# Two-layer hybrid encoder: the order of TensorE's matmuls through projections and branches

## The chip, the cores and the metric

The kernel runs on one core of a Trainium2 chip. The metric is device time in microseconds (us) of one execution. Each time is the median of several runs; a profile is one execution of the same program with the hardware profiler on.

## The reference

Two layers of a bidirectional encoder act on 272 tokens (16 meta tokens and 256 sequence tokens) of width 1024. Each layer projects the normalised tokens to four parallel mixers of width 256 and to a gate per mixer, adds the gated results, and goes through a feed-forward part of width 2816:

```python
for l in range(DEPTH):
    u = rms_norm(h, ln_mix[l])
    (aq, ak, av, bq, bk, bv, cq, ck, cv, dq, dzf, dzb, di, dg, gz) = split_in(u @ w_in[l])
    y_a = windowed_sink_attention(aq, ak, av, attn_sink[l], bias_a)
    y_b = axial_rope_attention(rms_norm(bq, qk_norm_q[l]), rms_norm(bk, qk_norm_k[l]), bv, row, col, key_ok)
    y_c = differential_attention(cq, ck, cv, lam, bias_c, key_ok, diff_subnorm[l], lam_init)
    y_d = hgrn2_bidirectional(dq, dzf, dzb, di, dg, lb_all[0, l], lb_all[1, l], valid, hgrn_out_norm[l])
    gate = sigmoid(gz).reshape(Bn, L, N_BRANCH, D_MODEL)
    merged = gate[:, :, 0] * (y_a @ w_branch[l, 0])
    for n, y in enumerate((y_b, y_c, y_d), start=1):
        merged = merged + gate[:, :, n] * (y @ w_branch[l, n])
    h = h + merged @ w_out[l]
    u = rms_norm(h, ln_ffn[l])
    h = h + (silu(u @ w_ffn_gate[l]) * (u @ w_ffn_up[l])) @ w_ffn_down[l]
return rms_norm(h, ln_final)[:, META_END:]
```

(Reshapes are left out.) Mixers a, b and c are softmax attentions with two key heads for four query heads; d is a gated linear recurrence that runs forwards and backwards. All values are float32.

## The kernel before, in words

**Tiles.** Activations are held transposed: 128 features on the partitions, 272 tokens along the row; a `slot` is 128 x 2 x 272. Weights come in blocks of 512 KB, 128 x 1024, in the order of the list `plan`. `split_next` (L258 to L279) issues the load of a block into `raw` on SP, ScalarE casts it to `whi` (L275), and VectorE writes the rest, raw minus `whi`, to `wlo` (L276). Activations are split into two parts in the same way. A product is then three matmuls, hi·a0, hi·a1 and lo·a0: `prod` (L290 to L292), or `prod_t` (L307 to L309) with the roles turned round, 512 columns at a time, in layer 1's gates and branch products. A column block, `block` (L294), is 8 such products or 24 matmuls into one PSUM tile of the pool `psm` (tiles `pmm`, four buffers). These are called the big matmuls here.

**Projections and branches.** A layer runs through 22 projections (`ORDER`, loop at L908), and then through gates and branch products (`MIXING` in layer 0, loop at L965; `mixing_t`, L830, in layer 1). Between these blocks stands the mixers' own work, written as two Python generators that `advance` (L900) takes one step further after each block:

- `branch_d` (L675) is the linear branch d. Its `close` (L690, matmuls L700 and L712) and `apart` (L718, L728) are many matmuls of 32 or 64 rows; then come L780 and L781, L794, L803, and at the end `mix` and `head_rstd`.
- `softmax_stream` (L623) does the branches c, b and a, for each query tile `scores` (L484, matmul L492), a softmax on VectorE and ScalarE, `turn` (L426, transposes L432 and L438), and per branch a `mix` (L410, matmuls L415 and L421). It lets `WAIT_C[l]` steps pass before it begins, and then waits for the branch's `ready`.

`values` (L388) transposes a projection of values (L395, and L404 for the meta tokens) and copies it to `vn` and `vm` (L396, L405); `prep_b` (L523) computes the norms of branch b's heads (`head_cols` L380, L541, `head_rstd` L371) and its rotation (L553); `mixing_t` ends each half with transposes of the sum `acc` (L868). All these use PSUM tiles of the pool `psa` (`pat`, four buffers).

**Order.** The program names its instructions in this order, with `values` and `prep_b` called right behind the projection that feeds them. A scheduler then orders each engine's instructions, by their place in the program and by when it expects their operands to be ready; the engines run that order as it stands, with waits on one another.

Of the kernel before, what the change touches and what calls it, by code (L numbers as in the profile page):

```python
# [15 lines left out]
P = 128  # L16
# [5 lines left out]
DEPTH = 2  # L22
# [20 lines left out]
BRANCHES = (3, 2, 1, 0)  # L43
AHEAD = 1
RATE_D, RATE_S = 1.0, 1.0
WAIT_C = (8, 8)


def mixing_order():
# [20 lines left out]
def first_token(l, name):  # L70

    return META if l == DEPTH - 1 and (name[1] in "qg" or name[:3] == "dzb") else 0
# [9 lines left out]
def trunk(ctx, tc, xT, w_in, w_branch, w_out, w_gate, w_up, w_down, rel_bias, params, consts, masks, onehot, ln_out, out):  # L82
    nc = tc.nc
    V, S, G, PE = nc.vector, nc.scalar, nc.gpsimd, nc.tensor

    one = ctx.enter_context(tc.tile_pool(name="one", bufs=1))
    wraw = ctx.enter_context(tc.tile_pool(name="wraw", bufs=5))
# [43 lines left out]
    def midt():  # L131
        return mid.tile([P, T], F32, tag="mid", name=nm("mid"))
# [694 lines left out]

    gl = ctx.enter_context(tc.tile_pool(name="gl", bufs=1))

    def mixing_t(acts, rcol, done, advance):  # L830

        gates, merged = {}, []
        acc = None
        for kind, b, half in MIXING_T:
            n = BRANCHES[b]
            if kind == "g":
                pss = [pmm(), pmm()]
                for x in range(4):
                    w = weights()
                    for k in range(2):  # L840
                        for i in range(2):
                            prod_t(pss[i], w, k * HALF, acts[2 * x + k], i, x + k == 0, x + k == 4)
                    advance(RATE_D, RATE_S)
                for i in range(2):
                    g = gates[n, half, i] = slot().rearrange("p a b -> p (a b)")[:, :HALF]
                    S.activation(out=g, in_=pss[i][:, :HALF], func=AF.Tanh, scale=rcol[:, i:i + 1])
                continue
            while n not in done:
                advance(1.0, 1.0)
            if acc is None:  # L850
                acc = accp.tile([P, KT, T], F32, tag="at", name=nm("acc")).rearrange("p a b -> p (a b)")[:, :2 * DM]
            w = weights()
            advance(RATE_D, RATE_S)
            for i in range(2):
                ps = pmm()
                for j in range(2):
                    prod_t(ps, w, j * HALF, done[n][j], i, j == 0, j == 1)
                g, a = gates[n, half, i], acc[:, DM * i + HALF * half:DM * i + HALF * (half + 1)]
                if b == 0:
                    V.scalar_tensor_tensor(out=a, in0=g, scalar=1.0, in1=ps[:, :HALF], op0=ALU.add, op1=ALU.mult)  # L860
                else:
                    V.scalar_tensor_tensor(out=g, in0=g, scalar=1.0, in1=ps[:, :HALF], op0=ALU.add, op1=ALU.mult)
                    V.tensor_tensor(out=a, in0=a, in1=g, op=ALU.add)
            if b == 3:
                for m in range(4 * half, 4 * half + 4):
                    ps = pat()
                    for i in range(2):
                        PE.transpose(ps[:, P * i:P * (i + 1)], acc[:, DM * i + P * m:DM * i + P * (m + 1)], ident)  # L868
                    t = slot(F32R)
                    S.copy(t[:, 0, META:], ps[:, :SEQ])  # L870
                    V.tensor_tensor(out=t[:, 1, META:], in0=ps[:, :SEQ], in1=t[:, 0, META:], op=ALU.subtract)
                    merged.append(t)
        return merged

    for l in range(DEPTH):
# [29 lines left out]
                    credit[x] -= 1.0  # L905
                    next(gen, None)

        for idx, name in enumerate(ORDER):  # L908
            t0 = first_token(l, name)
            ps = lead[idx] if idx < 3 else block(acts, t0)  # L910
            if l == 0 and idx == 3:
                prep_small()
            if name[:2] == "dz":
                d, j = name[2], int(name[3])
                z = midt()
                V.tensor_tensor(out=z[:, t0:], in0=ps[:, t0:T], in1=rstd[:, t0:], op=ALU.mult)
                dd = 0 if d == "f" else 1
                kdst, fdst = dt["KK"][:, 2 * dd + j, :], dt["T1"][:, 2 * (1 - dd) + j, :]
                if t0:
                    G.memset(kdst[:, :t0], 0.0)  # L920
                    G.memset(fdst[:, :t0], 1.0)
                fdst, kdst = fdst[:, t0:], kdst[:, t0:]
                S.activation(out=fdst, in_=z[:, t0:], func=AF.Sigmoid)
                S.activation(out=kdst, in_=z[:, t0:], func=AF.Sigmoid, scale=-1.0)
                if l > 0:
                    c = 2 * dd + j
                    V.tensor_scalar(out=fdst, in0=fdst, scalar1=lbc[:, c:c + 1], scalar2=lb[:, c:c + 1], op0=ALU.mult, op1=ALU.add)
                    V.tensor_scalar(out=kdst, in0=kdst, scalar1=lbc[:, c:c + 1], scalar2=None, op0=ALU.mult)
                V.tensor_scalar(out=fdst, in0=fdst, scalar1=1e-30, scalar2=None, op0=ALU.max)
                continue  # L930
            if name[0] == "d":
                dst = dt[name[1]][:, int(name[2]), :]
            else:
                half = 1 if name[1] == "v" or name[-1] == "1" else 0
                if half == 0:
                    cur = pj[name[:2]] = slot()
                dst = pj[name] = cur[:, half, :]
            scale = {"aq": 0.125, "cq": 32 ** -0.5, "dq": 0.125}.get(name[:2])
            if t0:
                G.memset(dst[:, :t0], 0.0)  # L940
            if scale is None:
                V.tensor_tensor(out=dst[:, t0:], in0=ps[:, t0:T], in1=rstd[:, t0:], op=ALU.mult)
            else:
                V.scalar_tensor_tensor(out=dst[:, t0:], in0=ps[:, t0:T], scalar=scale, in1=rstd[:, t0:], op0=ALU.mult, op1=ALU.mult)
            if name == "dg1":
                sg = gslot()
                S.activation(out=sg, in_=dt["g"], func=AF.Sigmoid)
                V.tensor_tensor(out=dt["g"], in0=dt["g"], in1=sg, op=ALU.mult)
            if name == "di1":
                dt["val", 3] = values([dt["i"][:, 0, :], dt["i"][:, 1, :]])  # L950
            if name[1] == "v":
                n = "abc".index(name[0])
                if n == 1:
                    prep_b(l, pj)
                    pj["b"] = parts_of(pj["bq"], pj["bk"])
                elif n == 2:
                    pj["c"] = parts_of(pj["cq"], pj["ck"], True)
                    if l == 0:
                        load_bias("a")
                pj["val", n] = values([pj[name]])  # L960
                pj["ready", n] = True
            advance(RATE_D if idx >= 8 else 0.0, RATE_S if idx >= 10 else 0.0)
        gates, merged = {}, []
        acc = w = None
        for kind, i, m in MIXING if l < DEPTH - 1 else ():  # L965
            n = BRANCHES[i]
            if kind == "g":

                if m % 2 == 0:
                    gates[n, m // 2] = slot()  # L970
                g = gates[n, m // 2][:, m % 2, c0:]
                ps = block(acts, c0)
                V.tensor_tensor(out=g, in0=ps[:, c0:T], in1=rstd[:, c0:], op=ALU.mult)  # L973
                S.activation(out=g, in_=g, func=AF.Tanh, scale=0.5)
                advance(RATE_D, RATE_S)
                continue
            while n not in done:
                advance(1.0, 1.0)
            if acc is None:
                acc = accp.tile([P, KT, T], F32, tag="at", name=nm("acc"))  # L980
            if m % 4 == 0:
                w = weights()
                advance(RATE_D, RATE_S)
            ps = pmm()
            for j in range(2):
                prod(ps, w, 2 * (m % 4) + j, done[n][j], c0, j == 0, j == 1)
            g = gates[n, m // 2][:, m % 2, c0:]
            if i == 0:
                V.scalar_tensor_tensor(out=acc[:, m, c0:], in0=g, scalar=1.0, in1=ps[:, c0:T], op0=ALU.add, op1=ALU.mult)
            else:  # L990
                t = midt()
                V.scalar_tensor_tensor(out=t[:, c0:], in0=g, scalar=1.0, in1=ps[:, c0:T], op0=ALU.add, op1=ALU.mult)
                V.tensor_tensor(out=acc[:, m, c0:], in0=acc[:, m, c0:], in1=t[:, c0:], op=ALU.add)
            if i == 3:
                merged.append(split_from(acc[:, m, :], c0, slot))
        if l == DEPTH - 1:
            merged = mixing_t(acts, rcol, done, advance)

            ws, pss = [weights(), weights()], [pmm(), pmm()]
            for k0 in (0, 4):  # L1000
# [195 lines left out]
```

## Time and profile before

| | |
|---|---|
| median of 3 runs | 924.46 us (923.78 to 926.39) |
| the profiled execution's own time | 924.85 us |
| its span in the profile | 923.1 us |
| its mean granted clock of TensorE | .995 |
| TensorE busy | 906.5 us (98%) |
| VectorE busy | 664.9 us (72%) |
| ScalarE busy | 505.1 us (55%) |

The span is what lies between the first and the last instruction of the profile. TensorE's rows are PE, its weight loads PEld, VectorE is DVE, ScalarE ACT, GpSimd POOL. `L395` is line 395 of the kernel; a row `pat L492 x6` is six matmuls of line 492 into tiles of the name `pat`. A number in brackets behind a row is idle time before it, with the instruction that ended it. The granted clock is a share of full speed.

### The profile page before, as it was taken

The numbers are of one execution on the slowest core, as the hardware profiler recorded it, in microseconds if no ns is written. First come the engines' busy times: TensorE is split into PE (matmuls) and PEld (weight loads), VectorE is DVE, ScalarE is ACT, GpSimd is POOL, SyncE is SP. The second block draws the span as 40 slices with busy tenths as digits, with TensorE's granted clock in tenths as the row PEclk, the third lists the DMA queues.
The fourth block names the chain that finished last, engine by engine and source line by source line (L and its number), as shares of the span: only waits on it lengthen the run. The fifth ranks groups of instructions, "written<-read, shape, count | busy, mean of one in ns | idle before, by whom it ended". The sixth has DMA issues, their size and how long they took to land.

```text
span 923.1 us, 18697 instructions
## 1 busy us (share of the span) xinstructions
PE 906.5 (98%) x7566; PEld 836.8 (91%) x7566; DVE 664.9 (72%) x1279; ACT 505.1 (55%) x852; POOL 23.5 (3%) x53
## 2 busy tenths in 40 slices
PE   7999999999999999999999999999999999999996
PEld 6988898999999999999999997787788999999885
DVE  7888886858987666665558888766577866777444
ACT  7645766555466444454446568675445655445432
POOL 1520000000000000000000000000000000000000
PEclk9999999999999999999999999999999999999998
DMA  8942344445454555555555423545465655555551
GB/s 314 247 145 77 108 138 138 137 138 158 140 183 161 182 174 171 181 171 174 182 176 168 150 82 115 166 132 162 157 195 152 201 182 173 189 186 184 186 179 45
DMA packets 42614, 150.04 MB, mean 163 GB/s; under 512 B 5024, under 2 KB 5696, under 8 KB 42528
## 3 DMA queue, kind: packets, MB, share of 16 engines
q1 hardware_dynamic: 40896, 144.84, 48.2%
q0 software_dynamic: 1344, 3.48, 1.5%
q8 instruction: 59, 0.97, 0.4%
q10 hardware_dynamic: 288, 0.52, 0.2%
q14 instruction: 27, 0.22, 0.1%
HBM read 147.22 MB, written 1.61 MB: 161 GB/s over the span
## 4 chain that ended last, share of the span: by engine, by line
PE 94%; DVE 3%; ACT 1%; issue 1%; DMA 1%; SPq 0%; DVEq 0%; ACTq 0%
PE pmm L290 22%; PE pmm L292 22%; PE pmm L291 22%; PE pmm L307 6%; PE pmm L309 6%; PE pmm L308 6%; PE pat L492 2%; PE pat L421 2%; PE pat L432 1%; DVE wlo L276 1%; ACT whi L275 1%; PE pat L700 1%; PE pat L371 1%; PE pat L415 1%; DMA h<-in_xT_dram 1%
## 5 line engine op out<-in xcount | busy, mean ns | idle before, releaser
L275 ACT CAST whi<-raw 128x1024 fp32r<-128x1024 f32 (+1 forms) x275 | 285.1, 1040 | 329.6 <-PE pmm L291 157.4
L290 PE MATMUL pmm<-slot,whi 128*128 128x272 f32 (+1 forms) x1552 | 449.8, 290 | 5.8 <-ACT slot L324 5.2
L291 PE MATMUL pmm<-slot,whi 128*128 128x272 f32 (+1 forms) x1552 | 446.2, 288 | 0.1
L292 PE MATMUL pmm<-slot,wlo 128*128 128x272 f32 (+1 forms) x1552 | 446.0, 288 | 0.1
L276 DVE TENSOR_TENSOR wlo<-raw,whi 128x1024 fp32r<-128x1024 f32 (+1 forms) x275 | 332.5, 1211 | 116.7 <-ACT whi L275 113.3
L290 PEld LDWEIGHTS pmm<-slot,whi 128*128 128x128 f32 x1552 | 293.5, 189 | 12.4 <-ACT slot L324 5.5
L291 PEld LDWEIGHTS pmm<-slot,whi 128*128 128x128 f32 x1552 | 294.2, 190 | 2.1 <-DVE slot L325 1.1
L292 PEld LDWEIGHTS pmm<-slot,wlo 128*128 128x128 f32 x1552 | 293.6, 189 | 1.9 <-issue 0.5
L307 PE MATMUL pmm<-whi,slot 128*128 128x512 f32 x184 | 73.2, 398 | 0.0
L309 PE MATMUL pmm<-wlo,slot 128*128 128x512 f32 x184 | 73.0, 397 | 0.0
L308 PE MATMUL pmm<-whi,slot 128*128 128x512 f32 x184 | 72.2, 392 | 0.0
L307 PEld LDWEIGHTS pmm<-whi,slot 128*128 128x128 f32 x184 | 34.6, 188 | 8.9 <-issue 1.2
L308 PEld LDWEIGHTS pmm<-whi,slot 128*128 128x128 f32 x184 | 34.6, 188 | 7.7
L309 PEld LDWEIGHTS pmm<-wlo,slot 128*128 128x128 f32 x184 | 34.6, 188 | 7.7 <-issue 0.3
L1030 DVE TENSOR_TENSOR mid<-pmm,rstd 128x272 f32<-128x272 f32 (+1 forms) x44 | 19.1, 433 | 27.0 <-PE pmm L292 26.9
L290 PE MATMUL pmm<-y,whi 128*128 128x272 f32 x128 | 37.2, 291 | 0.0
L292 PE MATMUL pmm<-y,wlo 128*128 128x272 f32 x128 | 36.9, 288 | 0.0
L291 PE MATMUL pmm<-y,whi 128*128 128x272 f32 x128 | 36.8, 288 | 0.0
L1026 DVE TENSOR_TENSOR mid<-pmm,rstd 128x272 f32<-128x272 f32 (+1 forms) x44 | 19.1, 433 | 17.4 <-PE pmm L292 17.2
L973 DVE TENSOR_TENSOR slot<-pmm,rstd 128x272 f32<-128x272 f32 x32 | 14.0, 439 | 16.3 <-PE pmm L292 16.1
L309 PE MATMUL pmm<-wlo,y 128*128 128x512 f32 x64 | 25.3, 396 | 0.0
L290 PEld LDWEIGHTS pmm<-y,whi 128*128 128x128 f32 x128 | 24.1, 188 | 1.3 <-issue 1.3
(261 smaller groups left out, 936.0 us busy)
## 6 DMA issues: line engine op xcount, KB each, us to landing
raw<-in_w_in_dram SPq DMA_DIRECT2D x106, 512.0 KB, 3.5
raw<-in_w_gate_dram SPq DMA_DIRECT2D x44, 512.0 KB, 3.3
raw<-in_w_up_dram SPq DMA_DIRECT2D x44, 512.0 KB, 3.4
raw<-in_w_down_dram SPq DMA_DIRECT2D x44, 512.0 KB, 3.3
raw<-in_w_branch_dram SPq DMA_DIRECT2D x16, 512.0 KB, 3.4
raw<-in_w_out_dram SPq DMA_DIRECT2D x16, 512.0 KB, 3.9
biasA<-scr POOLq DMA_DIRECT2D x8, 136.0 KB, 7.4
h<-in_xT_dram SPq DMA_DIRECT2D x3, 272.0 KB, 4.6
```

The costliest lines, as they stand in the source:

```text
L275: S.copy(hi[:, sl], raw[:, sl])
L276: V.tensor_tensor(out=lo[:, sl], in0=raw[:, sl], in1=hi[:, sl], op=ALU.subtract)
L290: PE.matmul(o, hi[:, sl], act[:, 0, c0:], start=first, stop=False)
L291: PE.matmul(o, hi[:, sl], act[:, 1, c0:], start=False, stop=False)
L292: PE.matmul(o, lo[:, sl], act[:, 0, c0:], start=False, stop=last)
L307: PE.matmul(o, a, hi[:, sl], start=first, stop=False)
L308: PE.matmul(o, b, hi[:, sl], start=False, stop=False)
L309: PE.matmul(o, a, lo[:, sl], start=False, stop=last)
L421: PE.matmul(ps[64 * hh:64 * hh + 64, c0:T], vn[:, i, vc:vc + 64], pT[i][:, hd, c0:], start=False, stop=i == 1, skip_group_check=True)
L492: PE.matmul(ps[:, :T], a[r, g, META + P * qt:META + P * (qt + 1)], b[r, :], start=n == 0, stop=n == 2)
L1026: V.tensor_tensor(out=g[:, c0:], in0=pg[:, c0:T], in1=rstd[:, c0:], op=ALU.mult)
L1030: V.tensor_tensor(out=u[:, c0:], in0=pu[:, c0:T], in1=rstd[:, c0:], op=ALU.mult)
```

## The change

TensorE alone is put under a manual schedule from the first projection to the end of the gates and products of both layers: its matmuls stay in the order in which the program names them. The other engines are ordered by the scheduler as before. `values` and `prep_b` are no longer called behind their projection; they are put on a list, `later`, which `catch_up()` empties right behind the next column block's matmuls. Branch b is `ready` once `prep_b` has been called. `WAIT_C` goes from (8, 8) to (11, 10), so that the softmax branches begin three and two steps later. No arithmetic, tile size or load is changed. Lines move by one from L85 on, and by more from L843 on (L868 becomes L870). The core of the difference, without the new indentation:

```diff
-WAIT_C = (8, 8)
+WAIT_C = (11, 10)
...
+    PE_ENGINE = mybir.EngineType.PE
...
                             prod_t(pss[i], w, k * HALF, acts[2 * x + k], i, x + k == 0, x + k == 4)
+                    catch_up()
                     advance(RATE_D, RATE_S)
...
+        with tc.manual_schedule(engines={PE_ENGINE}):
+            later = []
+            def take(n, tiles):
+                def f():
+                    (dt if n == 3 else pj)["val", n] = values(tiles)
+                later.append(f)
+            def take_b():
+                prep_b(l, pj)
+                pj["b"] = parts_of(pj["bq"], pj["bk"])
+                pj["ready", 1] = True
+            def catch_up():
+                while later:
+                    later.pop(0)()
         for idx, name in enumerate(ORDER):
             t0 = first_token(l, name)
             ps = lead[idx] if idx < 3 else block(acts, t0)
+            catch_up()
...
             if name == "di1":
-                dt["val", 3] = values([dt["i"][:, 0, :], dt["i"][:, 1, :]])
+                take(3, [dt["i"][:, 0, :], dt["i"][:, 1, :]])
             if name[1] == "v":
                 n = "abc".index(name[0])
                 if n == 1:
-                    prep_b(l, pj)
-                    pj["b"] = parts_of(pj["bq"], pj["bk"])
+                    later.append(take_b)
...
-                pj["val", n] = values([pj[name]])
-                pj["ready", n] = True
+                take(n, [pj[name]])
+                if n != 1:
+                    pj["ready", n] = True
...
                 ps = block(acts, c0)
+                catch_up()
...
-            merged = mixing_t(acts, rcol, done, advance)
+            merged = mixing_t(acts, rcol, done, advance, catch_up)
```

Three places show what moves in TensorE's order. The first is layer 0's first value transposes (L395, after: L396), with the linear branch's matmuls (`p`, `gk`) behind them; `pmm_847` and `pmm_837` are the same column block. Before:

```order
L290 MATMUL pmm_847<-slot_133,whi_712 128x272
L291 MATMUL pmm_847<-slot_133,whi_712 128x272
L292 MATMUL pmm_847<-slot_133,wlo_713 128x272
L395 MATMUL pat_782<-cst,slot_661 128x128 x2
L404 MATMUL pat_787<-cst,slot_661 32x64 x4
L700 MATMUL pat_795<-p_549,gk_793 32x32 x16
L700 MATMUL pat_813<-p_549,gk_793 32x32 x16
L712 MATMUL pat_831<-p_549,gk_793 32x16 x4
L290 MATMUL pmm_847<-slot_136,whi_712 128x272
```

After:

```order
L293 MATMUL pmm_837<-slot_153,wlo_715 128x272
L396 MATMUL pat_863<-cst,slot_663 128x128 x2
L405 MATMUL pat_868<-cst,slot_663 32x64 x4
L701 MATMUL pat_877<-p_551,gk_875 32x32 x16
L701 MATMUL pat_895<-p_551,gk_875 32x32 x16
L713 MATMUL pat_913<-p_551,gk_875 32x16 x4
L291 MATMUL pmm_929<-slot_123,whi_832 128x272
```

The visit has moved from behind the third of the block's eight products to behind the eighth (`slot_123` is the first operand of a block, `slot_153` the last).

The second is a pair of score visits in layer 0 (L492, after: L493; each writes two or four `pat` tiles). Before:

```order
L492 MATMUL pat_1487<-y_744,y_743 128x272
L492 MATMUL pat_1488<-y_744,y_743 128x272
L290 MATMUL pmm_1518<-slot_123,whi_1440 128x272
L291 MATMUL pmm_1518<-slot_123,whi_1440 128x272
L292 MATMUL pmm_1518<-slot_123,wlo_1441 128x272
L290 MATMUL pmm_1518<-slot_126,whi_1440 128x272
L492 MATMUL pat_1497<-y_744,y_743 128x272 x3
L291 MATMUL pmm_1518<-slot_126,whi_1440 128x272
L492 MATMUL pat_1498<-y_744,y_743 128x272 x3
L292 MATMUL pmm_1518<-slot_126,wlo_1441 128x272
```

After:

```order
L293 MATMUL pmm_1524<-slot_153,wlo_1458 128x272
L493 MATMUL pat_1561<-y_746,y_745 128x272
L493 MATMUL pat_1562<-y_746,y_745 128x272
...
L493 MATMUL pat_1571<-y_746,y_745 128x272
L493 MATMUL pat_1572<-y_746,y_745 128x272
...
L291 MATMUL pmm_1593<-slot_123,whi_1519 128x272
```

What were visits of six, three and three are now twelve in one piece (`...` stands for repeats) between two column blocks.

The third is layer 1's first eight output transposes (L868, after: L870). Before:

```order
L309 MATMUL pmm_8772<-wlo_8720,y_8403 128x512
L307 MATMUL pmm_8781<-whi_8719,y_8403 128x512
L868 MATMUL pat_8742<-cst,acc_8166 128x128
L868 MATMUL pat_8748<-cst,acc_8166 128x128
L868 MATMUL pat_8754<-cst,acc_8166 128x128
L868 MATMUL pat_8760<-cst,acc_8166 128x128
L308 MATMUL pmm_8781<-whi_8719,y_8403 128x512
```

After:

```order
L310 MATMUL pmm_8738<-wlo_8703,y_8444 128x512
L870 MATMUL pat_8747<-cst,acc_8154 128x128 x2
L870 MATMUL pat_8753<-cst,acc_8154 128x128 x2
L870 MATMUL pat_8759<-cst,acc_8154 128x128 x2
L870 MATMUL pat_8765<-cst,acc_8154 128x128 x2
L308 MATMUL pmm_8777<-whi_8724,y_8444 128x512
```

Before, seven matmuls of the next product (`pmm_8772` and one of `pmm_8781`) lie between the product that the transposes need and the transposes; after, none (`pmm_8738` is that product).

## Rows read from the trace of the kernel before

**Rows 1.** The page, part 1: busy time, share of the span, instructions of each engine.

```profile
PE 906.5 (98%) x7566; PEld 836.8 (91%) x7566; DVE 664.9 (72%) x1279; ACT 505.1 (55%) x852; POOL 23.5 (3%) x53
```

**Rows 2.** Stretches: us, busy (count) PE, PEld, DVE, ACT, POOL; clock, DMA share, GB/s.

```profile
51.98:56.00 4.02, 2.12 (x86) 1.56 (x84) 3.85 (x9) 0.49 (x2) 0.44 (x1) 0.79 0.34 125
56.00:60.00 4.00, 4.00 (x90) 3.83 (x91) 2.43 (x7) 1.86 (x3) 0.00 (x0) 0.78 0.42 131
60.00:97.00 37.00, 36.92 (x519) 32.05 (x517) 31.36 (x88) 20.90 (x42) 0.00 (x0) 1.00 0.27 87
232.00:500.00 268.00, 268.00 (x2135) 267.22 (x2133) 187.19 (x296) 134.72 (x194) 0.89 (x12) 1.00 0.53 172
```

**Rows 3.** Waits of TensorE, one of four: engine, tile, line, releaser: us, times, longest.

```profile
PE pat L395 <- DVE slot L942: 2.2, 2, 1.9
```

**Rows 4.** Timeline of TensorE, from 51.9 us: start us, us, engine line op, [idle before].

```profile
54.16 0.57 PE L395 MATMUL pat<-cst,slot 128*128 128x128 f32 x2 [1.90 <-DVE slot L942]
```

**Rows 5.** Chain of waits, 52 to 59 us: start us, us, what.

```profile
55.98 0.52 PE pmm L290
56.50 0.23 PE pmm L291
...
57.63 0.23 PE pmm L290
57.86 0.13 PE pmm L291
```

**Rows 6.** Chain of waits, score visits at 93, 97 and 134 us; one timeline row.

```profile
93.09 0.58 PE pat L492 x6
...
97.90 0.57 PE pat L492 x3
98.47 0.32 PE pmm L291
...
134.91 0.95 PE pat L492 x9
...
134.84 1.02 PE L492 MATMUL pat<-y,y 64*128 64x272 f32 x12
```

**Rows 7.** Chain of waits, 79.4 to 84.8 us, branch b's norms and values.

```profile
79.92 0.79 PE pat L380 x8
...
81.48 0.32 PE pmm L290
...
82.56 0.22 PE pat L395 x2
```

**Rows 8.** VectorE by line and form: busy us, mean ns, idle before and releasers.

```profile
L276 DVE TENSOR_TENSOR wlo<-raw,whi 128x1024 fp32r<-128x1024 f32 x270 | 329.6, 1223 | 115.9 <-ACT whi L275 112.6 <-PE pat L432 1.5
L434 DVE COPY pT<-pat 128x512 f32<-128x512 f32 x12 | 8.2, 685 | 1.6 <-PE pat L432 1.6
L863 DVE TENSOR_TENSOR acc<-acc,slot 128x512 f32<-128x512 f32 x12 | 8.0, 684 | 0.0
L333 DVE STREAM_TRANSPOSE turned<-pat 128x256 f32<-128x256 f32 x14 | 6.2, 446 | 5.7 <-PE pat L371 3.0 <-PE pat L351 2.6
L553 DVE SCALAR_TENSOR_TENSOR slot<-slot,par,cst 128x272 f32<-128x272 f32 x6 | 3.0, 494 | 0.0
L405 DVE TENSOR_TENSOR vm<-pat,cst 128x128 f32<-128x128 f32 x8 | 2.3, 285 | 0.7 <-PE pat L404 0.7
L314 DVE TENSOR_TENSOR y<-pat,y 128x272 fp32r<-128x272 f32 x4 | 1.8, 442 | 1.0 <-ACT y L313 1.0
```

**Rows 9.** Timeline of ScalarE, 79 to 83 us.

```profile
80.94 1.28 ACT L383 ACT_TABLE_LOAD   x1
82.24 0.27 ACT L383 ACTIVATE hr<-pat,cst 128x8 f32<-128x8 f32 x1
```

**Rows 10.** Chain of waits, 145 to 149 us, a mix of layer 0.

```profile
145.69 0.66 PE pat L415 x4
146.35 1.98 PE pat L421 x16
```

More of the change, by code (lines that the diff above doesn't have):

```diff
@@ L828, in trunk, with mixing_t @@
     gl = ctx.enter_context(tc.tile_pool(name="gl", bufs=1))
-    def mixing_t(acts, rcol, done, advance):
+    def mixing_t(acts, rcol, done, advance, catch_up):
         gates, merged = {}, []
@@ L906, in advance @@
                     next(gen, None)
[L908 to L918, printed above, removed]
-                if t0:
[L920 to L949, printed above, removed]
-                dt["val", 3] = values([dt["i"][:, 0, :], dt["i"][:, 1, :]])
-            if name[1] == "v":
-                n = "abc".index(name[0])
-                if n == 1:
-                    prep_b(l, pj)
-                    pj["b"] = parts_of(pj["bq"], pj["bk"])
[L956 to L959, printed above, removed]
-                pj["val", n] = values([pj[name]])
-                pj["ready", n] = True
-            advance(RATE_D if idx >= 8 else 0.0, RATE_S if idx >= 10 else 0.0)
@@ L963, in trunk @@
[L963 to L970, printed above, removed]
-                g = gates[n, m // 2][:, m % 2, c0:]
[L972 to L995, printed above, removed]
@@ new lines, in trunk @@
+        with tc.manual_schedule(engines={PE_ENGINE}):
[11 more added lines that the diff above has]
+                    later.pop(0)()
+            for idx, name in enumerate(ORDER):
+                t0 = first_token(l, name)
+                ps = lead[idx] if idx < 3 else block(acts, t0)
+                catch_up()
+                if l == 0 and idx == 3:
+                    prep_small()
+                if name[:2] == "dz":
+                    d, j = name[2], int(name[3])
+                    z = midt()
+                    V.tensor_tensor(out=z[:, t0:], in0=ps[:, t0:T], in1=rstd[:, t0:], op=ALU.mult)
+                    dd = 0 if d == "f" else 1
+                    kdst, fdst = dt["KK"][:, 2 * dd + j, :], dt["T1"][:, 2 * (1 - dd) + j, :]
+                    if t0:
+                        G.memset(kdst[:, :t0], 0.0)
+                        G.memset(fdst[:, :t0], 1.0)
+                    fdst, kdst = fdst[:, t0:], kdst[:, t0:]
+                    S.activation(out=fdst, in_=z[:, t0:], func=AF.Sigmoid)
+                    S.activation(out=kdst, in_=z[:, t0:], func=AF.Sigmoid, scale=-1.0)
+                    if l > 0:
+                        c = 2 * dd + j
+                        V.tensor_scalar(out=fdst, in0=fdst, scalar1=lbc[:, c:c + 1], scalar2=lb[:, c:c + 1], op0=ALU.mult, op1=ALU.add)
+                        V.tensor_scalar(out=kdst, in0=kdst, scalar1=lbc[:, c:c + 1], scalar2=None, op0=ALU.mult)
+                    V.tensor_scalar(out=fdst, in0=fdst, scalar1=1e-30, scalar2=None, op0=ALU.max)
+                    continue
+                if name[0] == "d":
+                    dst = dt[name[1]][:, int(name[2]), :]
+                else:
+                    half = 1 if name[1] == "v" or name[-1] == "1" else 0
+                    if half == 0:
+                        cur = pj[name[:2]] = slot()
+                    dst = pj[name] = cur[:, half, :]
+                scale = {"aq": 0.125, "cq": 32 ** -0.5, "dq": 0.125}.get(name[:2])
+                if t0:
+                    G.memset(dst[:, :t0], 0.0)
+                if scale is None:
+                    V.tensor_tensor(out=dst[:, t0:], in0=ps[:, t0:T], in1=rstd[:, t0:], op=ALU.mult)
+                else:
+                    V.scalar_tensor_tensor(out=dst[:, t0:], in0=ps[:, t0:T], scalar=scale, in1=rstd[:, t0:], op0=ALU.mult, op1=ALU.mult)
+                if name == "dg1":
+                    sg = gslot()
+                    S.activation(out=sg, in_=dt["g"], func=AF.Sigmoid)
+                    V.tensor_tensor(out=dt["g"], in0=dt["g"], in1=sg, op=ALU.mult)
+                if name == "di1":
+                    take(3, [dt["i"][:, 0, :], dt["i"][:, 1, :]])
+                if name[1] == "v":
+                    n = "abc".index(name[0])
+                    if n == 1:
+                        later.append(take_b)
+                    elif n == 2:
+                        pj["c"] = parts_of(pj["cq"], pj["ck"], True)
+                        if l == 0:
+                            load_bias("a")
+                    take(n, [pj[name]])
+                    if n != 1:
+                        pj["ready", n] = True
+                advance(RATE_D if idx >= 8 else 0.0, RATE_S if idx >= 10 else 0.0)
+            gates, merged = {}, []
+            acc = w = None
+            for kind, i, m in MIXING if l < DEPTH - 1 else ():
+                n = BRANCHES[i]
+                if kind == "g":
+                    if m % 2 == 0:
+                        gates[n, m // 2] = slot()
+                    g = gates[n, m // 2][:, m % 2, c0:]
+                    ps = block(acts, c0)
+                    catch_up()
+                    V.tensor_tensor(out=g, in0=ps[:, c0:T], in1=rstd[:, c0:], op=ALU.mult)
+                    S.activation(out=g, in_=g, func=AF.Tanh, scale=0.5)
+                    advance(RATE_D, RATE_S)
+                    continue
+                while n not in done:
+                    advance(1.0, 1.0)
+                if acc is None:
+                    acc = accp.tile([P, KT, T], F32, tag="at", name=nm("acc"))
+                if m % 4 == 0:
+                    w = weights()
+                    advance(RATE_D, RATE_S)
+                ps = pmm()
+                for j in range(2):
+                    prod(ps, w, 2 * (m % 4) + j, done[n][j], c0, j == 0, j == 1)
+                g = gates[n, m // 2][:, m % 2, c0:]
+                if i == 0:
+                    V.scalar_tensor_tensor(out=acc[:, m, c0:], in0=g, scalar=1.0, in1=ps[:, c0:T], op0=ALU.add, op1=ALU.mult)
+                else:
+                    t = midt()
+                    V.scalar_tensor_tensor(out=t[:, c0:], in0=g, scalar=1.0, in1=ps[:, c0:T], op0=ALU.add, op1=ALU.mult)
+                    V.tensor_tensor(out=acc[:, m, c0:], in0=acc[:, m, c0:], in1=t[:, c0:], op=ALU.add)
+                if i == 3:
+                    merged.append(split_from(acc[:, m, :], c0, slot))
+            if l == DEPTH - 1:
+                merged = mixing_t(acts, rcol, done, advance, catch_up)
```

## The prediction, on record before the changed kernel ran

> **What bounds the kernel now.** I read the page's first part, then a table of stretches, then what TensorE waited for, and last the chain of waits around each place where the change moves something. TensorE is busy 98% of the span, VectorE 72%, ScalarE 55% [rows 1]. In a steady stretch of 268 us, 2135 matmuls fill it without a gap, .1255 us from one start to the next, at the granted clock 1.00 [rows 2]: there only the number of matmuls counts, and the change keeps that number. What can be won or lost lies where TensorE stands still, where its clock falls, and where it leaves the big matmuls for a branch and comes back. The waits are few: for a value transpose (L395) on a tile that VectorE writes, 2.2 us in two times, the longer one 1.9 [rows 3]. It is the gap ahead of 54.16 [rows 4]. [...] The chain also shows the price of leaving: in it a score visit of six matmuls takes .58 and one of three .57, hardly less, and the first big matmul behind it .32 instead of .13 [rows 6]. One of twelve matmuls takes .95 (the chain names 9 pieces, the timeline 12 matmuls), and again .32 follows [rows 6]. A visit has a fixed price, mostly.
>
> **What the change removes.** Three things.
>
> (a) The wait of 1.90 [rows 4]. Before, the value transposes stand nine matmuls into the next block, on a tile that VectorE has just been asked for. After, they stand behind all 24 of that block, 15 matmuls or 15 × .1255 = 1.88 us [rows 2] later against the projection that feeds them. That covers the wait but for .02, so −1.90.
>
> (b) The low clock behind it [rows 5]. Six matmuls at .23 rather than .125: 6 × .105 = .63. The first one .52 rather than .32: .20. The two transposes .57 [rows 4], where the same pair takes .22 elsewhere [rows 7]: .35. Together −1.18.
>
> (c) The second such wait, 2.2 − 1.9 = .3: −.30.
>
> (d) Visits. In the order of matmuls TensorE leaves the big matmuls 91 times before and 76 times after (a run of other matmuls between two big ones counted as one visit): 15 fewer. The scores go from 25 pieces (of 1 to 12 matmuls) to 16 of 12. Beyond the step of .125 that the next big matmul takes anyway, a visit of 12 costs .95 + .32 − .125 = 1.145, one of 6 costs .58 + .32 − .125 = .775, one of 3 costs .57 + .32 − .125 = .765 [rows 6]. Two sixes made one twelve save .40; a three or a single that joins another visit saves about .77. I take five of the 15 at .77 (the threes, the single transposes) and ten at .40: 3.85 + 4.00 = −7.85. The ends are all at .40 (−6.0) and all at .77 (−11.55).
>
> Gains: 1.90 + 1.18 + .30 + 7.85 = **11.23**.
>
> **What the change adds.** TensorE now keeps the order in which the program names its matmuls, so where the next one is not ready nothing else steps in. No trace row shows these waits; each is worked out from what VectorE or ScalarE must do first, by durations of rows. The low end of each is 0 (the producer was early); the high end adds one weight split of 1.223 [rows 8] that VectorE has begun.
>
> 1. Layer 0, the visit with head_cols, head_rstd, values and the linear branch's last products: eight PSUM tiles in a row, four buffers. The transposes reuse the buffer that ScalarE's `hr` reads, and `hr` ends behind a weight cast and a table load of 1.28 at 82.24 + .27 = 82.51 [rows 9], 2.59 after the visit began at 79.92. TensorE's own pieces of the visit up to there take 79.92 to 81.48 = 1.56, and .22 for the transposes [rows 7]: 2.59 − 1.78 = **.81**.
> 2. The same visit in layer 1: the linear branch's products wait for a buffer behind VectorE's stream transpose .446, two operations of .494 and vm .285 [rows 8], 1.72, less .22 for the transposes and as much for the meta tokens' matmuls [rows 7]: **1.28**.
> 3. Layer 1, the last turn of a branch and its mix now follow each other with nothing between: VectorE's two copies, .685 and, for the 128 x 128 one, .285 as for vm [rows 8]: **.97**.
> 4. Layer 0's end: the last branch's mix and its product follow each other. VectorE owes two subtractions of .442 and may have two weight splits in front, 2 × .442 + 2 × 1.223 = 3.33 [rows 8]; the mix itself lasts .66 + 1.98 = 2.64 [rows 10]: **.69**.
> 5. Layer 1's first eight output transposes come right behind the product that they transpose. VectorE must still do a multiply with the gate and two sums of 128 x 512, 3 × .684 = 2.05 [rows 8], the multiply taken as long as the sum. Before, they stood seven matmuls into the next block. The second eight have five matmuls ahead of them: 2 × .684 − 5 × .1255 = .74. Together **2.79**.
> 6. Four visits of values followed by the linear branch's products want a fifth buffer, which vm's .285 frees [rows 8]: **1.14**.
>
> Waits: .81 + 1.28 + .97 + .69 + 2.79 + 1.14 = **7.68**. VectorE's and ScalarE's own work stays as it was; the later start of the softmax branches (11 and 10 steps rather than 8) costs nothing of its own while the matmuls of gates and products are there to cover it; if that cover is gone, the cost is waits 3 and 4. Loads: the weights keep their order, and their 27 to 53% of the transfer engines [rows 2] leave room.
>
> Sum: 7.68 − 11.23 = −3.55. The profiled execution took 924.85, so 921.30; it stands .39 above the median 924.46, so **920.9** for the median.
>
> On the table load, [rows 9] has `hr` starting .02 after the load's end, so I charge 1.28. [...]
>
> **The rivals.**
>
> A, no gain. The clock falls again, behind wait 5, the longest new one: after the old wait of 1.90 it had cost 1.18 [rows 5]. And a weight split of 1.223 stands ahead of VectorE's copies at waits 2 and 3. 920.9 + 1.18 + 2.45 = **924.5**. For it: a wait of 1.90 was enough to bring the clock down [rows 2, 4], and 2.05 is longer. Against it: a split in front of both is bad luck twice, since splits keep VectorE busy only 329.6 of 923 us [rows 8].
>
> B, slower: VectorE becomes the bound in the stretch of the softmax branches. From 60 to 97 us it is busy 31.36 of 37.00, 85% [rows 2]. The order before puts a branch's pieces among the big matmuls where they were expected to be ready; one that follows the program makes each of the 28 score and turn visits stand until its buffer is read. If each then waits for one small VectorE operation more, some .3 (vm's .285 [rows 8]), that is 28 × .3 = 8.4: **929.3**. At .13 a visit the gain is gone, at .23 it is slower by over .3%. Against it: the scores' visit now holds exactly the four buffers that are there, and a block of 3 us lies between two visits. [...]
>
> C, more gain: the blocks cover half of the new waits (−3.8): **917.1**.
>
> That the change does nothing is excluded: the order of matmuls differs at the places shown above.
>
> **How the numbers follow.** The forecast .45, C .13, A .22, B .20. A measurement of this kernel can tell about .3%, 2.8 us, from no change: faster is below 921.7, slower above 927.2. The forecast's own spread, some 919 to 923, lies on both sides of 921.7: I give .31 of it to faster and .14 to the same. With C's .13 faster is .44. A goes to the same but for .02: .34. B and the .02 make slower .22. The low end of the range, 915.5, lies under C by 1.6, part of the way to all 15 visits at .77 (3.7 lower); the high end, 928.5, takes in A with a split at all four waits (920.9 + 1.18 + 4.9 = 927.0) and B up to .28 a visit. Outside lies the heavier part of B and a gain on both ends at once.
>
> **What would show it.** Right: no wait at the value transposes and a granted clock of 1.00 from 52 to 60 us; score visits of 12 at .95; among TensorE's waits new rows for the output transposes on `acc` (about 2 us), for the layer 1 mix on pTm and for a PSUM tile behind `hr`. A falls if the clock stays at 1.00 after the output transposes. B shows as many short waits of score and turn matmuls, with VectorE at the other end, and as more than .125 from start to start between blocks in the softmax stretches. The forecast is wrong if the layer 0 stretch from 40 to 230 us is not shorter than before, for the visits it saves lie mostly there.

## The result: slower

| | us | ratio to before, 95% interval |
|---|---|---|
| before | 924.79 (923.78 to 926.39, 4 runs) | |
| changed | 932.85 (930.40 to 934.02, 4 runs) | 1.0082 (1.0069 to 1.0096) |

The forecast was 920.9 in a range of 915.5 to 928.5; the time lies above the range. Six more executions of the changed kernel in a later comparison gave 933.44 (ratio 1.0093, 1.0075 to 1.0111).

The changed kernel's page, part 1, answers to [rows 1]:

```profile
PE 902.9 (97%) x7566; PEld 834.1 (90%) x7566; DVE 665.8 (72%) x1279; ACT 499.1 (54%) x848; POOL 23.4 (3%) x53
```

TensorE does the same 7566 matmuls in 3.6 us less busy time than before, and the span grew from 923.1 to 928.6: what is lost is standing still. The stretches answer to [rows 2], same columns; the first takes the two of before together:

```profile
52.00:60.00 8.00, 6.65 (x189) 6.12 (x188) 8.00 (x18) 4.01 (x6) 1.62 (x2) 1.00 0.30 89
60.00:97.00 37.00, 36.10 (x517) 32.49 (x516) 30.05 (x81) 18.40 (x36) 0.00 (x0) 1.00 0.37 125
232.00:500.00 268.00, 267.81 (x2138) 265.22 (x2137) 186.39 (x297) 133.77 (x194) 0.89 (x12) 1.00 0.50 171
```

The clock is at 1.00 where it had been .79 and .78, as forecast, and the long stretch runs as before. TensorE's waits, whole, show where the time went. Before there were four, of 8.0 us together; 5.2 of them stood on the split of the activations (L324), which is the first row here too (L325):

```profile
PE pmm L291 <- ACT slot L325: 5.7, 3, 4.5
PE pat L439 <- DVE pmeta L437: 2.7, 4, 1.0
PE pat L870 <- DVE acc L865: 1.7, 2, 1.5
PE pat L493 <- DVE col L589: 1.4, 2, 0.8
PE pat L701 <- DVE p L758: 1.2, 1, 1.2
PE pat L795 <- DVE vm L406: 0.9, 1, 0.9
PE pmm L293 <- DVE wlo L277: 0.9, 1, 0.9
PE pat L405 <- ACT hr L384: 0.9, 1, 0.9
PE pat L416 <- DVE pTm L440: 0.9, 1, 0.9
PE pat L433 <- ACT p L460: 0.6, 1, 0.6
PE pmm L292 <- DVE y L315: 0.2, 1, 0.2
```

Without the first row these are 11.4 us, against 2.8 before. The row of [rows 3] is gone, as forecast. The waits on `acc`, `vm`, `hr`, `pTm` and `y` were on the list of the forecast; `pmeta`, `col`, `wlo`, ScalarE's `p` and the linear branch's `p L758` were not.

The longest unlisted row, `pmeta`, read at 118 us. VectorE's timeline (start, us, what):

```profile
118.32 0.36 DVE L462 TENSOR_SCALAR p<-p,col 128x272 f32<-128x272 f32 x1
118.59 1.22 DVE L277 TENSOR_TENSOR wlo<-raw,whi 128x1024 fp32r<-128x1024 f32 x1
119.73 0.43 DVE L995 TENSOR_TENSOR slot<-pmm,rstd 128x272 f32<-128x272 f32 x1
120.08 0.22 DVE L437 COPY pmeta<-p 128x128 f32<-128x128 f32 x1
```

and TensorE's:

```profile
118.85 1.03 PE L433 MATMUL pat<-cst,p 128*128 128x128 f32 x8
120.35 0.33 PE L439 MATMUL pat<-cst,pmeta 128*128 128x128 f32 x1 [0.46 <-DVE pmeta L437]
```

A copy of .22 us that could start at 118.7 stands behind a weight split of 1.22 and a scaling of .43, because the scheduler still chooses VectorE's order; TensorE, which may not go on, waits for it. At the output transposes a weight split stands in the way only in part. VectorE:

```profile
698.96 1.23 DVE L277 TENSOR_TENSOR wlo<-raw,whi 128x1024 fp32r<-128x1024 f32 x1 [1.65 <-ACT whi L276]
700.10 1.34 DVE L864 SCALAR_TENSOR_TENSOR slot<-slot,pmm 128x512 f32<-128x512 f32 x2
701.36 1.29 DVE L865 TENSOR_TENSOR acc<-acc,slot 128x512 f32<-128x512 f32 x2
```

and TensorE:

```profile
702.19 0.30 PE L870 MATMUL pat<-cst,acc 128*128 128x128 f32 x1 [1.47 <-DVE acc L865]
702.70 0.98 PE L870 MATMUL pat<-cst,acc 128*128 128x128 f32 x7 [0.21 <-DVE acc L865]
```

The product's last big matmul starts at 700.32 and takes .40, so VectorE's second multiply and its sum, some 1.3 us, could not be done before some 702.0 even without the split (an estimate from these rows); that much of the wait is the work itself, as the forecast had it. No split stands ahead of `vm` at 550 us and `pTm` at 628 us either. What these waits share is that TensorE has matmuls behind them that are ready and may not run, as experiment 1 shows.

Behind this wait the clock falls, in this execution. The stretch, columns as in [rows 2]:

```profile
703.90:707.30 3.40, 3.40 (x10) 2.65 (x9) 2.51 (x6) 0.37 (x2) 0.00 (x0) 0.51 0.48 154
```

The big matmuls of 512 columns stand .43 apart there instead of .23, which makes some 1.6 us.

### The profile page after: what moved, and what is told of

It reads as the page before. It is cut to its first block, busy times and chain, and to the rows that moved or that the text cites. A ratio compares the mean times of both kernels' runs of the same rounds, so it can differ in the third digit from the quotient of the medians.

```text
span 928.6 us, 18685 instructions
## 1 busy us (share of the span) xinstructions
PE 902.9 (97%) x7566; PEld 834.1 (90%) x7566; DVE 665.8 (72%) x1279; ACT 499.1 (54%) x848; POOL 23.4 (3%) x53
## 4 chain that ended last, share of the span: by engine, by line
PE 86%; DVE 8%; ACT 3%; issue 2%; DMA 1%; SPq 0%; DVEq 0%; ACTq 0%
PE pmm L291 21%; PE pmm L292 20%; PE pmm L293 20%; PE pmm L308 6%; PE pmm L310 6%; PE pmm L309 6%; DVE wlo L277 2%; PE pat L422 1%; PE pat L493 1%; ACT whi L276 1%; PE pat L433 1%; PE pat L701 1%; DMA h<-in_xT_dram 1%; ACT p L593 1%; PE pat L416 0%
## 5 line engine op out<-in xcount | busy, mean ns | idle before, releaser
L308 PE MATMUL pmm<-whi,y 128*128 128x512 f32 x64 | 25.9, 404 | 0.0
```

What stands on the lines that cost most here:

```text
L308: PE.matmul(o, a, hi[:, sl], start=first, stop=False)
```

## The experiments

Theory 1: the fixed order of TensorE makes the loss, since it stands behind small operations of VectorE that the scheduler places behind weight splits. Theory 2, the rival: the later start and the deferred calls push the softmax branches out from under their cover. All edits are against the changed kernel unless another is named; each comparison ran beside the kernel before on the same chip. The comparisons ran on different chips (the kernel before has medians of 923.95 to 925.25 on them), so times of different comparisons are set against each other by their ratios to it as well.

A number is used below that stands in no view as it is. A **visit's cost** is the time from the start of the last big matmul before it to the start of the first one behind it, less one step (.124 us; .117 for 256 columns, .231 for 512). Summed over all visits it is 100.1 us before, 105.0 in the changed kernel.

**1. The manual schedule taken out** (`e1_no_manual`).

```diff
-        with tc.manual_schedule(engines={PE_ENGINE}):
+        with ExitStack():
```

> The changed kernel with the manual schedule of TensorE taken out; the deferred values and the later start stay. Theory 1 (the fixed order of TensorE makes it stand behind small operations of VectorE that the scheduler still places behind weight splits): the waits on pmeta, vm, pTm, acc and col, 10 us in the changed kernel's profile, go, and the time is 921 to 926. Theory 2 (the later start and the deferral push the softmax branches out from under their cover): it stays at 930 or more.

Measured: 918.40 (917.87 to 918.52), ratio .9938 (.9923 to .9953), before 923.95. The same program with a free order is faster than both kernels, and below the 921 to 926 that theory 1 had; the fixed order costs 932.85 − 918.40 = 14.45, or 13.3 by the ratios. Its waits, whole:

```profile
PE pmm L291 <- ACT slot L325: 5.8, 2, 4.4
PE pat L701 <- DVE p L758: 1.3, 1, 1.3
PE pmm L291 <- ACT whi L276: 0.4, 1, 0.4
PE pat L433 <- ACT p L460: 0.3, 1, 0.3
```

How little the two orders differ is the point. Visits number 86 against 76, and their cost is 94.6 against 105.0. The difference of 10.4 lies in ten places, where the free order lets a piece slip behind a few big matmuls: turn visits at 118, 170, 217 and 577 us (.71, 1.77, 1.30, .64), the visits with `hr` and with `vm` (1.09, .91), values followed by scores (.31, .51), the turn with its mix (1.02), the output transposes (2.13); 10.4 together. The two profiled executions differ by 930.40 − 918.52 = 11.9, so these places and the 1.6 of the clock behind the output transposes are nearly all of it. The chain at the first of these, in the run without the manual schedule:

```profile
117.01 0.87 PE pat L433 x8
117.89 0.13 PE pmm L291
...
119.25 0.12 PE pmm L293
119.38 0.16 PE pat L439
119.53 0.13 PE pmm L291
```

Twelve big matmuls run between the eight transposes and the ninth, and that ninth adds .16 to the chain, itself included. The two visits cost .88 together, and behind the second return one more step is .09 longer (.21 from start to start); nine transposes in one piece without a wait cost .90 (the visit at 134 us of the changed kernel). So going back and forth costs under .1 us, and it saves .71. VectorE is no earlier here. The transposes and the copy, from the timelines of both engines in this run:

```profile
116.85 1.04 PE L433 MATMUL pat<-cst,p 128*128 128x128 f32 x8
118.93 0.22 DVE L437 COPY pmeta<-p 128x128 f32<-128x128 f32 x1
```

The copy starts 2.08 us after the transposes begin, in the changed kernel 1.23 (120.08 and 118.85). The copy is later still and no wait on it is left in this run, since twelve big matmuls run in the meantime.

**2. The start after 8 steps again** (`e2_wait_8_8`): `WAIT_C = (11, 10)` becomes `(8, 8)`.

> The changed kernel with the softmax branches started after 8 steps again in both layers. Theory 1: the waits stay, 930 to 936. Theory 2: the visit in which a turn and a mix follow each other uncovered goes, and the time is 925 to 928.

Measured: 934.22 (931.88 to 937.04), 1.0112 (1.0083 to 1.0140). The waits stay: without the row of the split they are 11.7 us, though part of them under other names. With experiment 1, where the start is late and the calls are deferred as in the changed kernel, theory 2 falls.

**3. The manual schedule alone** (`e3_manual_alone`): as in 2, and the deferral undone.

```diff
-                later.append(f)
+                f()
...
-                        later.append(take_b)
+                        take_b()
```

> The manual schedule alone: values and prep_b called at once again, the start after 8 steps. Theory 1: slower than the changed kernel by the values' own waits, four times some 2 us: 936 to 942. Theory 2: as fast as the kernel before, 923 to 928.

Measured: 942.74 (941.52 to 944.40), 1.0198 (1.0181 to 1.0215), just above what theory 1 has. The first row of its waits shows what the deferral is for under a fixed order; the free order of the kernel before has 2.2 of it [rows 3]:

```profile
PE pat L396 <- DVE slot L963: 6.4, 8, 2.3
```

**4. The manual schedule in layer 0 alone** (`e4_manual_layer0`).

```diff
-        with tc.manual_schedule(engines={PE_ENGINE}):
+        with tc.manual_schedule(engines={PE_ENGINE}) if l == 0 else ExitStack():
```

> The changed kernel with the manual schedule in layer 0 alone. In its profile layer 0 lost 0.8 us and layer 1 3.7 us against the kernel before, so theory 1 expects 927 to 930; theory 2, where the manual schedule does not matter, 932 to 933.

Measured: 926.20 (923.45 to 927.99, 10 runs), 1.0022 (1.0012 to 1.0033). A little below the expected range: the fixed order costs 7.8 in layer 0 and, in layer 1, 6.7 by the medians and 5.5 by the ratios.

**5 and 6. Single waits covered, the manual schedule kept.** In `e5_transposes_later` the loop over `m` that transposes `acc` moves to a function, called for the first half after the second half's products and for the second half between the two `k0` of the next blocks. In `e6_pmeta_early` the copy is named a step earlier:

```diff
             next(gen, None)
+            pm = None
+            if qt is not None:
+                pm = two.tile([P, 4, 32], F32, tag="pmeta", name=nm("pmeta"))
+                V.tensor_copy(pm, st["p"][:, :, 0:32])
             yield
```

> The changed kernel, manual schedule kept, with layer 1's output transposes named one product later, the second eight behind the first half of the next blocks. If the fixed order loses by what it puts ahead of its cover, the wait on acc (1.7 us in two) and the cost of its two visits (3.7 us) fall to about 1 us, and with them the clock's fall behind them: 929 to 931. If the cost lies elsewhere and a wait just moves: 932 to 934.

Measured: 931.13 (930.24 to 932.88), 1.0069 (1.0054 to 1.0084). The wait on `acc` is gone; 1.0 of the 1.7 comes back as waits on the transposes' own splits (`slot L877` .7, `slot L876` .3). The time is 1.7 less than the changed kernel's by the medians, 1.2 by the ratios, whose intervals overlap: a gain is not shown.

> The changed kernel, manual schedule kept, with the copy pmeta named one step earlier, right behind the softmax's division, so that VectorE has it done a block before TensorE wants it. If the waits on pmeta (2.7 us in four) are lost time, 929 to 931; if TensorE then waits for the next small copy instead, 932 to 934.

Measured: 928.68 (927.81 to 929.86), 1.0041 (1.0026 to 1.0056). 4.2 less than the changed kernel by the medians, 3.8 by the ratios, for one small copy named earlier, and a little below the expected range. Its row of 2.7 is down to .3, which is 2.4 of it; the mean clock of these four executions was .992 to .996, that of three of the changed kernel's four .990 to .991, so the rest is probably clock.

**7. All of them covered, the manual schedule kept** (`f1_manual_covered`): 5 and 6, `WAIT_C = (11, 9)`, and one deferred call per block:

```diff
-                while later:
+                if later:
                     later.pop(0)()
```

> Manual schedule kept, every long wait of the changed kernel given a cover: pmeta and the output transposes as in the two runs before, one deferred call per block so that norms and values stand in different visits, layer 1's start after 9 steps so that a turn and a mix are a block apart. If the fixed order loses only by those waits, the sum of them falls from 11.2 to 3 us or less and the time is 919 to 924; if new waits come in their place, 925 to 929.

Measured: 927.07 (922.84 to 927.94, 10 runs), 1.0013 (.9999 to 1.0028). The waits fell from 11.4 to 6.4; the visits cost 99.4. What the fixed order lost can be won back by hand, to about the time of before, but some waits do come in their place. Its two largest rows are the start's and one that had been .6:

```profile
PE pmm L291 <- ACT slot L325: 5.6, 2, 4.6
PE pat L433 <- ACT p L458: 2.0, 2, 1.4
```

**8. The same edits without the manual schedule** (`f2_free_with_edits`).

> The run without the manual schedule, with pmeta and the output transposes named as in the two runs before. These edits won 4.2 and 1.7 us under the fixed order. If it is the fixed order that made them needed, nothing changes here: 917 to 919.5. If they are gains of their own: 912 to 915.

Measured: 920.42 (919.43 to 921.28), .9956 (.9941 to .9971). Under a free order the edits that won 4.2 and 1.7 win nothing. By the ratios they cost .2%, some 1.7 us, though the intervals overlap. A wait on the transposes' splits of .7 us (`slot L879`) is one part of that; two of the four executions had a mean clock of .998 and took 919.4 and 919.7, two had .995 and .996 and took 921.1 and 921.3.

**9. VectorE in program order as well** (`f4_manual_vector_too`).

```diff
-        with tc.manual_schedule(engines={PE_ENGINE}):
+        with tc.manual_schedule(engines={PE_ENGINE, mybir.EngineType.DVE}):
```

> The changed kernel with VectorE in program order as well. If TensorE waited because the scheduler put weight splits ahead of small copies, the copies come first now, the waits on pmeta, vm and pTm go, and the time is 924 to 929. If VectorE then stands at products that are not ready and holds the weight splits back, TensorE waits for wlo, and the time is over 935.

Measured: 1018.61 (1012.17 to 1020.05), 1.0995 (1.0955 to 1.1034). Its three longest waits:

```profile
PE pat L795 <- DVE p L788: 20.6, 2, 10.5
PE pmm L293 <- DVE wlo L277: 19.6, 11, 4.5
PE pat L439 <- DVE pmeta L437: 12.2, 12, 1.8
```

The weight splits are late, as the second case had it, and `pmeta` got no better. Putting the second engine in program order too is no way out.

**10. Deferral and later start by themselves, free order.** `e7_deferral_alone` is 1 with `WAIT_C = (8, 8)`; `e8_start_alone` is the kernel before with `WAIT_C = (11, 10)`.

> No manual schedule and the start after 8 steps: the kernel before with values and prep_b deferred by a block. If the deferral makes all of the gain of the run without the manual schedule (5.5 us): 917 to 919.5. If the later start makes half of it: 920 to 922.

Measured: 925.20 (921.85 to 928.18, 10 runs), .9999 (.9984 to 1.0013): nothing, against the expectation.

> The kernel before with the softmax branches started after 11 and 10 steps, nothing else. If the deferral makes the gain: 923 to 925, as before. If the later start makes half of it: 920.5 to 922.

Measured: 923.13 (922.29 to 924.80, 10 runs), .9982 (.9973 to .9992): some 2 us. So neither part alone makes the gain of 5.5; together they do. The trace of the deferral alone shows where some of it went: the softmax's scores stand close behind the linear branch's last products, and TensorE's clock goes down. Stretches of that run (columns as in [rows 2]), then two more, cut where the clock falls:

```profile
88.00:94.70 6.70, 6.70 (x39) 4.89 (x38) 3.51 (x15) 1.47 (x3) 0.00 (x0) 0.72 0.01 2
94.70:101.50 6.80, 6.80 (x38) 4.09 (x37) 3.52 (x9) 4.09 (x11) 0.00 (x0) 0.77 0.47 154
101.50:108.30 6.80, 6.80 (x55) 5.61 (x54) 4.99 (x17) 5.49 (x15) 0.00 (x0) 1.00 0.11 34
88.00:91.00 3.00, 3.00 (x24) 2.42 (x23) 1.41 (x6) 0.42 (x1) 0.00 (x0) 1.00 0.02 5
91.00:97.80 6.80, 6.80 (x30) 4.02 (x31) 4.04 (x10) 4.14 (x9) 0.00 (x0) 0.50 0.17 57
```

and its chain there:

```profile
93.82 1.21 PE pat L416 x4
95.03 3.38 PE pat L422 x16
```

The mix of .66 + 1.98 [rows 10] takes 1.21 + 3.38. In the run of both parts, the first three stretches read 1.00. The early start by itself did not bring the clock down: the kernel before has it too, with scores even in the visit of those products, and its trace reads 1.00 from 60 to 97 us [rows 2]. At an equal mean clock of .997 the deferral alone took 921.85 and 922.46, against a median of 924.4 of eight executions of the kernel before in the same comparison, and the later start alone 922.74 to 922.92: 2.2 and 1.7 less. So most of the 5.5 is the sum of the two.

**11. A still later start, free order** (`f3_free_start_12_11`): 1 with `WAIT_C = (12, 11)`.

> The run without the manual schedule, softmax branches after 12 and 11 steps rather than 11 and 10. If a still thinner mixture of branch work keeps helping: 916 to 918; if the tail of the last branch loses its cover, which the order shows (a transpose visit and the mix of layer 0 now follow each other): 919 to 922.

Measured: 919.05 (918.78 to 919.40), .9941 (.9927 to .9956): at the low end of the second case, no better than 11 and 10.

**12. The last wait of the free order** (`g1_free_parts_later`): 1 with branch c's `parts_of` named three blocks later.

> The run without the manual schedule, with branch c's split queries and keys (parts_of, five operations of VectorE) moved from behind its own projection to three blocks later. The one wait left among the branches, 1.3 us of the linear branch's matmuls on VectorE's p, stands behind that split. If it is lost time: 916.5 to 917.5; if another operation of VectorE takes the place: 918 to 919.

Measured: 918.76 (918.17 to 919.37), .9939 (.9927 to .9952): nothing. The wait of 1.3 on `p L758` is now one of 1.1 on ScalarE's `whi`; it moved.

**13. The changed kernel once more** (`g2_changed_again`).

> The changed kernel once more, for a second trace and more runs. If the 2.4 us between its profiled execution (930.4, clock .995) and its other runs (clock .990 to .991) are the clock, runs at a mean clock of .995 or more take 929 to 931 and runs at .991 or less take 932 to 934; if they are waits of varying length, time and clock do not go together.

Time and mean clock of its six executions: 929.22 at .995; 933.40 at .993; 932.37, 933.48, 935.11 and 935.12 at .991. With the four of the first comparison (930.40 at .995; 932.76, 932.94 and 934.02 at .990 to .991) they go together: 929 to 930 at the higher clock, 932 to 935 at the lower. So some 3 us of a typical run are clock, on top of the waits. Apart from the last microseconds the two profiled executions have one fall each, at different places: behind the output transposes at 703.9 in the first, at 88.3 in this one. Six traces of the fixed order (experiments 2, 4 to 7 and 13) have a fall that begins between 85.8 and 90.2, within 3 us of the wait on `hr`; the first trace has the same wait and no fall there, so why it comes in some executions and not in others stays open.

## Why the prediction was wrong, point by point

- **(a), (b), (c), the value transposes.** Right as far as they went: no wait there, clock 1.00 from 52 to 60 us. But (a) counted the whole 1.90 as won, and the linear branch's matmuls of the same stretch then waited 1.2 for VectorE's `p`. The net is −.7 rather than −1.9, and moving VectorE's work away from there (experiment 12) only changed the name of that wait.
- **(d), −7.85 for 15 fewer visits: mis-sized.** The free order of the same program makes its visits for 94.6 instead of 100.1, which is 5.5 less. Of that, (a), (c) and the transposes' .35 of (b) are 2.55, and waits inside its own visits give 1.6 back, so fewer visits are worth 5.5 − 2.55 + 1.6 = 4.55, some 60%, and five fewer (91 to 86) were enough for it. The ten more that the fixed order saves come with 10.4 us of cost. "A visit has a fixed price" was read from score visits, of 64 rows, and priced at .77 and .40. A full-size transpose slipped in between adds .16 at most (experiment 1), and five of the ten visits that the fixed order saved were of full-size transposes alone, four of turns and one of the output.
- **New waits, 7.68.** Those listed came, 4.6 instead of 7.68: `hr` .9 (forecast .81), `pTm` .9 (.97), `vm` .9 (1.28), `acc` 1.7 (2.79), `y` .2 (.69), the fifth buffer 0 (1.14). The list was the error: `pmeta` 2.7, `p L758` 1.2, `col` 1.4, `wlo` .9 and `p L460` .6 stood on no line of it, 6.8 together. **The failed step is the first sentence of that part, "where the next one is not ready nothing else steps in", applied to six places that the order showed as crowded and not to the turn visits**, which look the same in both orders but for one slip of a few matmuls. What the runs showed in its place: with the order fixed TensorE waits 11.4 us behind late operations of VectorE and ScalarE, with it free and all else alike 2.0. The sign that the prediction named for being wrong came too: from the linear branch's first visit to the end of layer 0 (before 42.84 to 283.64, after 44.15 to 285.71) the changed kernel takes 241.6 us against 240.8, so it is not shorter.
- **The rivals.** B had the mechanism and the side: many visits wait for a small VectorE operation. It priced 28 visits at .3; the score and turn visits waited 2.7 + 1.4 + .6 = 4.7, .17 each, and the waits of the other places came on top. B's 929.3 is close to the changed kernel at the higher clock, 929.2 and 930.4, but by luck: B sets gains of 11.23 against waits of 7.68 + 8.4 = 16.08, where the rows have gains of some 6.2 (3.2 in visits, .8 in big matmuls, 2.2 in old waits) and waits of 11.4. Its reading of why was off: VectorE was not the bound (30.05 of 37 us, less than before), its order was, a copy of .22 behind a split of 1.22. A's clock came too, and in the profiled execution where A had it, behind the output transposes: some 1.6 us instead of 1.18. Elsewhere it came without them, as at 88.3 in the second trace.
- **Ready matmuls behind a wait.** Of the 10.4 us in the ten places, 8.7 are rows of waits (10.3 inside visits, 1.6 in the free order), with ready matmuls behind. In the trace of the changed kernel none of them ran in the .46 before 120.35 and the 1.47 before 702.19. The wait on `hr` is .9, as the forecast's .81 had it with the table load charged at 1.28: in the trace of the kernel before, ScalarE's next instruction starts within .02 us of the end of each of the 23 table loads after the first, of 1.28 each.
- **The sum.** Forecast −3.55. By the rows: visits without their waits (105.0 − 10.3) − (100.1 − 2.2) = −3.2, the big matmuls of (b) −.8, waits 11.4 − 2.8 = +8.6, the split of the activations +.5; that is +5.1 of the profiled executions' 930.40 − 924.85 = 5.55. Two further terms partly cancel: the clock behind the output transposes, +1.6, and the longer step behind each return to the big matmuls, −1.0 with 15 fewer returns; with them the sum is 5.7. The clock of the other executions, 2 to 3 us more, makes the 8 of the medians.

## What to carry to other kernels

Before pinning an engine's order, list what each of its instructions waits for and where the scheduler has put that on the other engines: here TensorE, pinned, waited 11.4 us behind late operations of VectorE and ScalarE, which were not, against 2.0 without the pin, and the list of visits did not show it, since the slips that avoid it are a few instructions long. Take the edit apart first: here the two edits to the program were worth −5.5 us together under the free order, and the pin turned them into +8. The version to keep is experiment 1, 918.4 against 924.0, both edits without the pin.

## What had not been expected of the hardware

- **The clock fell in a stretch without a wait.** In the run of the deferral alone TensorE was busy throughout from 88.00 to 97.80 us; the clock was 1.00 until 91.00 and .50 from there on. What it had done before the fall was the linear branch's last products and two visits of three scores, with three big matmuls between them. The run of both parts kept 1.00 in these stretches, and so did the kernel before, which has much the same work there. Of ten executions of the deferral alone, the two with a mean clock of .997 took 921.85 and 922.46, those at .992 925.5 to 928.2. What brought the clock down was not tried by itself and stays open.
- **The price of leaving the big matmuls differed with what for.** In the chain, one full-size transpose between big matmuls adds .16 us, and the first big matmul behind it takes .13 as any other (experiment 1). Three score matmuls of 64 rows add .57, and the first big matmul behind them takes .32, .765 in all [rows 6].
